# Expert results in two buffers per half of the columns, 31 instead of 32 weight slots, and the last pair stored by 256 columns

## The chip, the core and the metric

The kernel runs as one program on one core of a Trainium2 chip. The core has a matrix engine (TensorE, PE in the profile, with its weight loads as PEld), three engines for elementwise work (VectorE or DVE, ScalarE or ACT, GpSimd or POOL) and SyncE (SP), whose queue issues the DMA transfers here. Matmul operands are read from SBUF and results land in PSUM, which has eight banks. The metric is the device time of one execution in microseconds, lower is better.

## What is computed

One layer of a diffusion backbone over 512 latent tokens of 1024 features: a token mixer (neighbourhood attention beside a bidirectional RWKV-7 scan), then a mixture of 32 experts, of which each token uses two. The change is in the expert part:

```python
combine = jnp.sum(jax.nn.one_hot(expert_id, N_EXPERTS, dtype=jnp.float32) * top_w[..., None], axis=1)
out = jnp.zeros_like(hf)
for e in range(N_EXPERTS):
    he = jax.nn.silu(hf @ w1[e]) * (hf @ w3[e])
    out = out + combine[:, e:e + 1] * (he @ w2[e])
...
x = x + mod_x[5] * hier_moe(...)
```

Here `w1[e]` and `w3[e]` are 1024 by 512 and `w2[e]` is 512 by 1024, all float32, so each expert has 6 MB of weights, which are read once.

## The kernel before, in words

Each expert has a room of 64 tokens. `moe_phase` (line 1541) runs 16 pairs of experts, `moe_pair` for each. The two experts of a pair fill 128 rows, 64 each. For every second pair `gather` (1743) collects the features of four experts: TensorE multiplies one-hot matrices `OH` by the tokens (`pga`), and ACT moves the banks to `HS`. Pair 0 finds much of its gather already done.

A pair then runs so. The first products with `w1` and `w3` go to two PSUM banks (`ph`, 64 matmuls in the profile's count). ACT computes `hid = silu(ph)` and DVE multiplies it by the second bank, line 1798. TensorE transposes it (`pth`), and ACT copies it to `hT`. `turned` (1837) makes the pair's scatter matrix `oht` and its weights `cs` from a table (`pbp`, `pbc`). The products with `w2` (`py`) come in two halves of 512 columns. For each half `result` (1853) has DVE multiply by `cs` and the gate to `yv` (a tile `HS` for half 0, `hid` for half 1), ACT round it to `yh`, and DVE compute the rest `yl = yv - yh`, so that the two together carry float32 through matmuls in a shorter format. `scatter` (1864) multiplies `oht` by `yh` and `yl` for each of four token tiles (`psc`, eight matmuls for a half) and DVE adds the bank to the residual `x`. The pool `PM` has one buffer for each name, so one `yh` and one `yl`; both halves use them.

The scatter of a pair is a generator, `s.todo`, which the next pair advances: half 0 (four steps, line 1799) behind that pair's product `hid`, half 1 (line 1805) behind `hT`. So TensorE runs: `ph` of the next pair, scatter of half 0, `pth`, scatter of half 1, `pbp`/`pbc`, `py`. TensorE and DVE keep the order in which the program is written in this stage, as do the weight loads on SP; ACT's order is set by a scheduler.

Weights come by `wload2` (1708), two transfers of 512 KB at a time. There are `sum(RING)` slots in six pools, taken in turn, so load n takes the slot of load n - 32 and waits until TensorE has used it; it also waits for the load eight before it. The last pair (`e == 30`) takes its columns in four parts of 256, and `scatter` stores finished columns of `x` when the last token tile of a part is added and the part's end is a key of `STORES`: two transfers for each store, one for each half of the rows of the grid.

Of the kernel before, what the change touches and what calls it, by code (L numbers as in the profile page):

```python
# [9 lines left out]
F32R = mybir.dt.float32r  # L10
# [180 lines left out]
OUT_ORD = ('scalar',)  # L191
MOE_ORD = ('vector',)
LAST_PARTS = (256, 256, 256, 256)
STORES = {512: 0, 768: 512, 1024: 768}
PEND = 8.32  
AHEAD = 4
LATE = (4, 8, 12)
RING = (6, 15, 3, 4, 2, 2)
EARLY = 6


# [25 lines left out]
class K:  # L227
# [1480 lines left out]
    def wload2(s, e, m, b):  # L1708

        two = []  # L1710
        for h in range(2):
            n = s.nload % sum(RING)
            s.nload += 1
            r = next(r for r in range(len(RING)) if n < sum(RING[:r + 1]))
            src = s.A[m][e + h, b]
# [57 lines left out]
    def moe_pair(s, PM, e, batch):  # L1773

        nc = s.nc
        q = e // 2 % 2
        last = e == 30
        if q == 0:
            OH, s.HS, begun = batch
            if s.HS is None:  # L1780
                s.HS = s.features_room(PM)
            s.all(s.gather(OH, s.HS, begun))
        HS = s.HS[:, :, 128 * q:128 * q + 128]
        hs = [slice(64 * h, 64 * h + 64) for h in range(2)]
        hh = []
        for m in ('w1', 'w3'):
            ph = s.ps(tag='ip', name="ph")
            for b in range(4):
                ws = s.wload2(e, m, b)
                for k in range(2):  # L1790
                    kt = 2 * b + k
                    for h in range(2):
                        s.mm(ph[hs[h], :], HS[:, kt, hs[h]], ws[h][:, k], kt == 0, kt == KT - 1)
            hh.append(ph)
        ws = [s.wload2(e, 'w2', b) for b in range(4)]
        hid = PM.tile([128, 512], F32, name="hid")
        s.act(hid, hh[0], AF.Silu)
        nc.vector.tensor_tensor(hid, hid, hh[1], ALU.mult)
        s.some(s.todo, 4)
        pt = s.ps(tag='nt', name="pth")  # L1800
        for f in range(4):
            s.tr(pt[:, 128 * f:128 * f + 128], hid[:, 128 * f:128 * f + 128])
        hT = PM.tile([128, 512], F32, name="hid").rearrange("p (a b) -> p a b", a=4)
        s.act(hT.rearrange("p a b -> p (a b)"), pt)
        s.all(s.todo)
        oht, cs = s.turned(PM, e, HS[:, 4:8])
        batch = (s.moe_batch(PM, e // 4 + 1), None, None) if q and not last else None

        c0 = 0
        parts = LAST_PARTS if last else (512, 512)  # L1810
        for z, n in enumerate(parts):
            c = slice(c0, c0 + n)
            d = slice(c0 % 512, c0 % 512 + n)
            py = s.ps((128, n), tag=('ip', 'ip', 'rm', 'nt')[z], name="py")
            for a in range(c0, c0 + n, 256):
                for f in range(4):
                    for h in range(2):
                        s.mm(py[hs[h], a - c0:a - c0 + 256], hT[:, f, hs[h]], ws[a // 256][h][:, f], f == 0, f == 3)
            if d.start == 0:
                y2 = [PM.tile([128, 512], F32R, name=x) for x in ("yh", "yl")]  # L1820
            yh, yl = [t[:, d] for t in y2]

            yv = HS[:, c0 // 128:(c0 + n) // 128] if last or z == 0 else PM.tile([128, 512], F32, name="hid").rearrange("p (a b) -> p a b", a=4)
            s.result(yv, py, cs, s.mod5[c0 // 512][:, d], yh, yl)
            if last:
                s.all(s.todo)
            new = s.scatter(oht, c, yh, yl, last)
            s.todo = new if last or z == 0 else s.chain(s.todo, new)
            c0 += n
        s.all(s.todo) if last else None  # L1830
        return batch
# [32 lines left out]
    def scatter(s, oht, c, yh, yl, last=False):  # L1864

        for i in range(4):
# [5 lines left out]
            s.nc.vector.tensor_tensor(x, po, x, ALU.add)  # L1872
            if last and i == 3 and c.stop in STORES:
                s.store(slice(STORES[c.stop], c.stop))
            yield
# [119 lines left out]
```

## Time and profile before

| | us |
|---|---|
| Median of 3 runs (lowest, highest) | 1272.22 (1269.41, 1273.02) |
| Profiled execution, its time | 1272.23 |
| Its span in the trace | 1270.4 |
| TensorE matmul busy | 1133.3 (89%) |
| TensorE weight loads busy | 775.4 (61%) |
| DVE busy | 660.3 (52%) |
| ACT busy | 393.6 (31%) |
| GpSimd busy | 253.3 (20%) |

The expert stage begins at about 722 us of the span. The shares are means over stages of different kinds, so they don't tell what bounds this stage; that is read from its own waits and its timeline. Where an engine is idle, the profile names what it was waiting for. All instructions that a helper records have one line number (242 for matmuls, 212 for most others), so rows are told apart by their tiles, as `out<-in`. Times of matmuls overlap: one starts before the one ahead of it has ended.

### The profile page before, as it was taken

The numbers are of one execution on the slowest core, as the hardware profiler recorded it, in microseconds if no ns is written. First come the engines' busy times: TensorE is split into PE (matmuls) and PEld (weight loads), VectorE is DVE, ScalarE is ACT, GpSimd is POOL, SyncE is SP. The second block draws the span as 40 slices with busy tenths as digits, with TensorE's granted clock in tenths as the row PEclk, the third lists the DMA queues.
The fourth block names the chain that finished last, engine by engine and source line by source line (L and its number), as shares of the span: only waits on it lengthen the run. The fifth ranks groups of instructions, "written<-read, shape, count | busy, mean of one in ns | idle before, by whom it ended". The sixth has DMA issues, their size and how long they took to land.

```text
span 1270.4 us, 23663 instructions
## 1 busy us (share of the span) xinstructions
PE 1133.3 (89%) x9545; PEld 775.4 (61%) x9546; DVE 660.3 (52%) x1461; ACT 393.6 (31%) x743; POOL 253.3 (20%) x277
## 2 busy tenths in 40 slices
PE   4899998997968989999979899999999999998995
PEld 2677766865737868887757545454645545454644
DVE  5745597598899335544787513333333231313335
ACT  3533534545444446553223401020111101010101
POOL 0655364544343100202350300000000000000000
PEclk9999988996889889999989899999999999999998
DMA  9434634744534786643438599999989899999932
GB/s 368 152 125 146 196 130 132 203 143 128 139 109 147 198 239 195 197 101 105 122 119 346 177 410 406 376 367 367 405 330 410 328 395 367 369 361 375 354 155 68
DMA packets 148221, 309.98 MB, mean 244 GB/s; under 512 B 32260, under 2 KB 70020, under 8 KB 148109
## 3 DMA queue, kind: packets, MB, share of 16 engines
q1 hardware_dynamic: 143324, 306.08, 67.9%
q10 hardware_dynamic: 4752, 2.36, 0.6%
q8 instruction: 76, 1.25, 0.4%
q14 instruction: 37, 0.30, 0.1%
q0 software_dynamic: 32, 0.00, 0.0%
HBM read 283.22 MB, written 25.17 MB: 243 GB/s over the span
## 4 chain that ended last, share of the span: by engine, by line


## 5 line engine op out<-in xcount | busy, mean ns | idle before, releaser
L242 PE MATMUL ph<-wt,HS 128*64 128x512 f32 x1024 | 222.9, 593 | 0.0
L212 DVE TENSOR_TENSOR yl<-hid,yh 128x512 fp32r<-128x512 f32 x15 | 10.4, 692 | 287.8 <-ACT yh L212 287.8
L242 PEld LDWEIGHTS ph<-wt,HS 128*64 128x64 f32 x1024 | 72.9, 137 | 139.3 <-issue 131.0
L242 PE MATMUL py<-wt,hid 128*64 128x256 f32 x1024 | 114.7, 381 | 0.0
L212 POOL CAST two<-sel 128x128 fp32r<-128x128 f32 x32 | 8.5, 293 | 495.6 <-PE pbc L242 490.2
L242 PEld LDWEIGHTS py<-wt,hid 128*64 128x64 f32 x1024 | 71.9, 137 | 41.4 <-issue 6.3
L212 POOL TENSOR_TENSOR wlo<-wraw,whi 128x512 fp32r<-128x512 f32 x54 | 74.5, 1382 | 71.5 <-ACT whi L212 69.6
L242 PE MATMUL ipn<-whi,hth 128*128 128x256 f32 x256 | 80.2, 313 | 5.8 <-DVE vs L212 4.6
L212 ACT ACTIVATE yh<-hid 128x512 fp32r<-128x512 f32 x15 | 9.4, 629 | 243.8 <-PE psc L242 243.8
L212 DVE TENSOR_TENSOR x<-psc,x 128x512 f32<-128x512 f32 (+1 forms) x136 | 79.9, 649 | 1.5
L242 PE MATMUL ip<-hth,whi 128*128 128x512 f32 (+1 forms) x200 | 75.9, 380 | 0.3 <-ACT nr L212 0.2
L242 PE MATMUL ipn<-wlo,hth 128*128 128x256 f32 x256 | 75.4, 295 | 0.0
L242 PE MATMUL ipn<-whi,htl 128*128 128x256 f32 x256 | 75.3, 294 | 0.0
L242 PE MATMUL ip<-htl,whi 128*128 128x512 f32 (+1 forms) x200 | 72.6, 363 | 0.7 <-DVE htl L212 0.7
L242 PE MATMUL ip<-hth,wlo 128*128 128x512 f32 (+1 forms) x200 | 72.2, 361 | 0.0
L242 PE MATMUL psc<-yh,oht 128*128 128x512 f32 (+1 forms) x136 | 67.0, 496 | 1.3 <-DVE x L212 0.9
L242 PE MATMUL psc<-yl,oht 128*128 128x512 f32 (+1 forms) x136 | 63.6, 471 | 0.0
L242 PEld LDWEIGHTS ipn<-whi,hth 128*128 128x128 f32 x256 | 52.2, 204 | 17.7 <-issue 14.7
L242 PE MATMUL pga<-OH,xl 128*128 128x256 f32 x240 | 60.2, 291 | 2.2 <-POOL xl L212 2.2
L242 PE MATMUL pga<-OH,xh 128*128 128x256 f32 x240 | 61.0, 294 | 1.0 <-DVE OH L212 1.0
L212 DVE TENSOR_TENSOR tmp<-Mc,Tc 128x30 f32<-128x30 f32 (+14 forms) x120 | 54.2, 452 | 4.7 <-ACT Tc L212 3.2
L212 DVE TENSOR_TENSOR Tc<-Tc,tmp 128x30 f32<-128x30 f32 (+14 forms) x120 | 52.4, 436 | 2.0
(352 smaller groups left out, 2291.0 us busy)
## 6 DMA issues: line engine op xcount, KB each, us to landing
wt<-in_w_dram SPq DMA_DIRECT2D x384, 512.0 KB
wm<-in_wmod_dram SPq DMA_DIRECT2D x48, 512.0 KB
wraw<-in_w_in_dram SPq DMA_DIRECT2D x30, 256.0 KB
wraw<-in_w_na_dram SPq DMA_DIRECT2D x24, 256.0 KB
BKj<-BKd SPq DMA_DIRECT2D x12, 512.0 KB
BKd<-BK SPq DMA_DIRECT2D x12, 384.0 KB
ARz<-ARd SPq DMA_DIRECT2D x16, 256.0 KB
wo<-in_w_out_dram SPq DMA_DIRECT2D x16, 256.0 KB
```

The costliest lines, as they stand in the source:

```text
L212: i = f(*a, **k)
L242: i = s.nc.tensor.matmul(out, l, r, start=start, stop=stop)
```

## The change

`yh` and `yl` get two buffers each, so that half 0 and half 1 alternate between them. The room comes from the fourth pool of weight slots, which has three slots instead of four, so load n waits for load n - 31. `STORES` gets a key for column 256, so that the first 512 columns are stored in two parts.

```diff
-STORES = {512: 0, 768: 512, 1024: 768}
+STORES = {256: 0, 512: 256, 768: 512, 1024: 768}
...
-RING = (6, 15, 3, 4, 2, 2)
+RING = (6, 15, 3, 3, 2, 2)
...
             if d.start == 0:
-                y2 = [PM.tile([128, 512], F32R, name=x) for x in ("yh", "yl")]
+                y2 = [PM.tile([128, 512], F32R, name=x, bufs=2) for x in ("yh", "yl")]
```

The rows of TensorE, DVE and GpSimd come in the same order as before. On ACT, the order around a gather in the expert stage was this before (`yh<-HS` is half 0's rounding, `yh<-hid` is half 1's, `hid<-ph` is Silu and `hid<-pth` the copy to `hT`):

```order
L212 ACTIVATE hid<-pth 128x512
L212 ACTIVATE yh<-HS 128x512
L212 ACTIVATE HS<-pga,modv,sc_6889 128x256 x8
L212 ACTIVATE yh<-hid 128x512
L212 ACTIVATE hid<-ph 128x512
```

In the changed kernel the same place on ACT reads:

```order
L212 ACTIVATE hid<-pth 128x512
L212 ACTIVATE yh<-HS 128x512
L212 ACTIVATE yh<-hid 128x512
L212 ACTIVATE HS<-pga,modv,sc_6889 128x256 x8
L212 ACTIVATE hid<-ph 128x512
```

The rounding of half 1 has moved ahead of the eight moves of gathered features. This is so at all seven gathers behind pair 0.

On SP, the end of the expert stage (the last two weight loads, the stores, and the check whether an expert has more than 64 tokens) differs so:

```order
 L212 DMA wt_11671<-in_w_dram 128x1024
 L212 DMA wt_11673<-in_w_dram 128x1024
-L212 DMA out_dram<-x_4959 64x4x512 x2
-L212 DMA out_dram<-x_4959 64x4x256 x4
+L212 DMA out_dram<-x_4959 64x4x256 x8
 L1881 TENSOR_LOAD cmax
 L1882 COMPARE_AND_BRANCH
```

Two stores of 512 columns have become four of 256; they stay behind all weight loads.

## Rows read from the trace of the kernel before

**Rows 1.** page, 40 slices of the span: GB/s that the DMA engines moved in each

```profile
GB/s 368 152 125 146 196 130 132 203 143 128 139 109 147 198 239 195 197 101 105 122 119 346 177 410 406 376 367 367 405 330 410 328 395 367 369 361 375 354 155 68
```

**Rows 2.** waits, 722 to 1262: engine, line, waited for; us in total, times, longest

```profile
PE pth L246 <- DVE hid L212: 39.4, 16, 2.9
...
PEld ph L242 <- DMA wt<-in_w_dram: 3.4, 12, 0.3
```

**Rows 3.** timeline, one pair: start us, us, engine; in brackets idle before, releaser

```profile
896.58 0.50 PE L242 MATMUL psc<-yh,oht 128*128 128x512 f32 x1
...
898.83 0.63 ACT L212 ACTIVATE yh<-hid 128x512 fp32r<-128x512 f32 x1 [17.88 <-PE psc L242]
...
899.49 0.69 DVE L212 TENSOR_TENSOR yl<-hid,yh 128x512 fp32r<-128x512 f32 x1 [15.75 <-ACT yh L212]
...
900.22 0.60 ACT L212 ACTIVATE hid<-ph 128x512 f32<-128x512 f32 x1 [0.76 <-DVE yl L212]
...
900.85 0.69 DVE L212 TENSOR_TENSOR hid<-hid,ph 128x512 f32<-128x512 f32 x1 [0.66 <-ACT hid L212]
...
901.45 1.88 DVE L212 TENSOR_TENSOR x<-psc,x 128x512 f32<-128x512 f32 x3
...
901.59 0.66 PE L246 MATMUL pth<-cst,hid 128*128 128x128 f32 x4 [2.90 <-DVE hid L212]
```

**Rows 4.** windows: us; PE, PEld, DVE, ACT, POOL busy; granted clock, DMA share, GB/s

```profile
901.60:902.60 1.00, 0.96 (x5) 0.70 (x6) 1.00 (x2) 0.32 (x1) 0.00 (x0) 0.96 1.01 401
902.70:905.90 3.20, 3.20 (x9) 2.54 (x8) 3.06 (x7) 0.18 (x1) 0.00 (x0) 0.50 1.02 408
906.10:940.00 33.90, 31.34 (x204) 18.37 (x203) 7.69 (x14) 5.93 (x11) 0.53 (x2) 1.00 0.92 363
722.00:1257.80 535.80, 495.46 (x2856) 272.11 (x2855) 175.26 (x288) 70.69 (x125) 7.96 (x30) 0.95 0.88 345
```

**Rows 5.** timeline, pair 0

```profile
729.22 0.60 ACT L212 ACTIVATE hid<-ph 128x512 f32<-128x512 f32 x1 [4.67 <-PE ph L242]
...
735.95 0.66 PE L246 MATMUL ptb<-cst,byt 128*128 128x128 f32 x4
...
736.89 0.66 PE L246 MATMUL pth<-cst,hid 128*128 128x128 f32 x4 [0.29 <-DVE hid L212]
```

**Rows 6.** waits of SP's DMA queue, 722 to 1257

```profile
SPq L212 <- PE ph L242: 114.9, 83, 8.9
...
SPq L212 <- PE py L242: 110.4, 51, 8.8
```

**Rows 7.** windows of the weight stream

```profile
658.30:735.00 76.70, 68.22 (x447) 47.47 (x449) 50.84 (x189) 29.87 (x58) 16.90 (x21) 0.90 0.71 268
...
735.00:765.00 30.00, 26.53 (x157) 12.32 (x153) 7.85 (x12) 3.08 (x6) 0.53 (x2) 1.00 1.03 410
...
1219.50:1257.80 38.30, 35.65 (x216) 19.11 (x213) 16.14 (x32) 3.70 (x7) 0.00 (x0) 0.96 0.00 1
...
658.30:1219.50 561.20, 515.02 (x3027) 296.09 (x3029) 209.97 (x446) 93.96 (x172) 24.86 (x51) 0.94 0.92 360
```

**Rows 8.** page, DMA issues: count, KB each

```profile
wt<-in_w_dram SPq DMA_DIRECT2D x384, 512.0 KB
```

**Rows 9.** timeline, last pair and stores

```profile
1224.34 13.90 PE L242 MATMUL ph<-wt,HS 128*64 128x512 f32 x64
...
1252.74 1.41 DVE L212 TENSOR_TENSOR x<-psc,x 128x256 f32<-128x256 f32 x4
...
1255.58 1.95 PE L242 MATMUL py<-wt,hid 128*64 128x256 f32 x16
...
1257.85 1.36 SPq L212 DMA_DIRECT2D out_dram<-x  x2
...
1259.05 2.73 DVE L212 TENSOR_TENSOR x<-psc,x 128x256 f32<-128x256 f32 x8
...
1263.64 1.98 SPq L212 DMA_DIRECT2D out_dram<-x  x2
```

## The prediction

> **What bounds the kernel now.** I start with the slices of the page [rows 1]. Slices 24 to 38 are mostly the expert stage, in which the weight loads move some 330 to 410 GB/s. The first question is whether TensorE or the weight stream sets the pace there. The waits of that stage answer it [rows 2]: the matmul side of TensorE stood for 39.4 us, 16 times, before the transposes `pth` of the hidden tile, and its weight loads stood for only 3.4 us because weights had not landed. The queue that issues the loads, on the other hand, waited 225 us for TensorE to give slots back [rows 6]. So weights are early, and TensorE is the bound, with one hole per pair.
>
> The timeline of one pair shows the hole [rows 3]. TensorE starts the scatter of half 0 at 896.58, and `pth` at 901.59 after 2.90 us without work, so the eight scatter matmuls are over at 898.69. In it four instructions run one after another: ACT `yh` of half 1 (898.83), DVE `yl` (899.49), ACT's Silu into `hid` (900.22), DVE's product `hid` (900.85, 0.69 long). ACT had waited 17.88 us for `psc` by then: the one `yh` buffer was still read by half 0's scatter, which TensorE runs only after the next pair's 64 `ph` products. DVE keeps program order, so the product stood behind `yl`.
>
> The windows by clock show a second cost [rows 4]. A microsecond behind the hole the clock falls to 0.50 (the 1.2 GHz level of the two): 902.7 to 905.9 reads 0.50, the microsecond before it 0.96, the stretch from 906.1 to 940 reads 1.00. TensorE is busy all through the slow stretch, 3.20 of 3.20 us, so the fall adds half of its length to the chain.
>
> **The change, part by part.** *Two buffers for `yh` and `yl`.* Half 1 no longer takes the buffer that half 0's scatter reads; its own was last read by the previous pair's half-1 scatter, before the `py` products that feed it. `yh` and `yl` then run right behind `py`, under 13.90 us of `ph` products [rows 9]. ACT can take Silu as soon as the w1 products end, half way through `ph`. What is left behind `ph` is the product `hid` alone. Pair 0, which has no scatter in front of it, already runs like that [rows 5]: Silu at 729.22, in the middle of `ph`; TensorE's next work (four other transposes) at 735.95, and `pth`, which still waits for the product, at 736.89: 0.94 us after `ph`. In later pairs the eight scatter matmuls cover 2.11 us, which hides 0.94 with 1.17 to spare. The cover would hold even if Silu came late (0.60 more).
>
> So 15 of the 16 holes go; pair 0 keeps its 0.29 us [rows 5]. 39.4 - 0.3 = **39.1 us**. The fall of the clock comes 15 times, each behind a hole; by the windows it is between 3.2 and 3.5 us long, I take 3.4. Half of 3.4 times 15 is **25.5 us**. As a check, a mean clock of 0.95 over 535.8 us [rows 4] is a loss of 26.8, within the rounding of that figure. I take the fall to go with its hole, as nothing else in the stage precedes one; if it doesn't, the price is a rival below.
>
> *What is late next?* After `pth` the half-1 scatter needs the banks that DVE's additions empty: DVE starts them 0.9 us behind `ph`, at 0.63 each (1.88 for three [rows 3]), and bank i is free at about 1.6+0.63i; TensorE asks for it at about 2.8+0.46i, so by the fourth pair of matmuls the margin is still 0.7 us. I cost this at nothing; if it fails, it costs at most some 0.7 us per pair.
>
> *ACT's new order.* Where a gather follows, `yh` of half 1 stands ahead of the eight `HS` evacuations. It needs only `py` and DVE, and TensorE hardly waits for `HS` at all, so I cost it at nothing. The upper end is 0.63 x 7 = 4.4 us, if in each of the seven gathers behind pair 0 every `HS` came late by a whole `yh` and TensorE waited for it.
>
> *One slot less (31 instead of 32).* Each load waits for a slot one load younger. In the trace of before that costs nothing: the last weights land at 1219.5 (from then on 1 GB/s) [rows 7] and the last `py` group starts at 1255.58 [rows 9], 36 us later. With TensorE faster, it matters. A load is 512 KB [rows 8], and at the 410 GB/s of 735 to 765 [rows 7] takes 1.279 us; 24 of them need 30.7 us per pair. TensorE's time per pair was 34.2 us (ten pairs from 896.58 [rows 3] to the end of the last `ph` at 1238.24 [rows 9], five of them with a gather) and falls by 2.6 + 1.7 to 29.9, so the lead shrinks by 0.8 us per pair. The tightest place is the last pair's `ph`: its end at 1238.24 [rows 9] moves by 14 x (2.61+1.70) to 1177.9, and its last eighth, which needs load 376 of 384, starts at 1176.2. Until 735, 268 GB/s x 76.7 us [rows 7] is 39 loads, of which I count 38 as landed; 735 + 338 x 1.279 + 1.28 for the lost slot is 1168.6. The lead left is 7.6 us, so the slot costs nothing, but the margin is thin: the stream must hold (1176.2-735-1.28)/338 = 1.302 us per load, **403 GB/s**. The lower bound of the slot's price is nothing, the upper a load per pair, 15 x 1.28 = 19 us, if the stream is the bound throughout; as the row gives 410, I take the lower.
>
> *Stores of the last pair.* Eight of 256 KB instead of two of 512 and four of 256. The first two are free to go when the additions of the first 256 columns end, 1252.74+1.41, instead of 1257.85 [rows 9]. SP has issued all loads by then. Before, the last two issues began at 1263.64, though the last additions ended at 1261.78: SP's queue was behind. With 512 KB gone 3.7 us earlier the last two can start between 1261.8 and 1263.6: a gain of nothing to 1.9 us. I take **1.5 us**, near the upper end, since the queue then has a quarter of its bytes behind it.
>
> Sum, against the profiled execution of 1272.23 us (span 1270.4; the median of the runs shown is 1272.22, so no correction): 39.1 + 25.5 + 1.5 = 66.1, which gives **1206.1 us**.
>
> **The rivals.**
> *The half-level clock stays.* Something else than the hole could bring it down, the change to `psc` and `pth` shapes for one. Against it: one fall per hole, and none around pair 0. Time: 1206.1 + 25.5 = 1231.6. Chance 0.06.
>
> *The stream becomes the bound.* Then the hole moves from `pth` to the weights of the last pairs. For it: the mean over 658.3 to 1219.5 is only 360 GB/s [rows 7], and the margin above is 2%. Against it: the stream was held back by slots for 225 us of that time [rows 6], and unhindered it went at 410. At 360 GB/s (1.456 us), 346 loads after 735 end at 1238.8; from the last group's start at 1255.58 to the end are 16.7 us, less 1.5 for the stores: 1254. Near the margin, at 391 GB/s (1.341 us), it is 1214. Chance 0.07 for more than 1218. The Trainium skill (DMA: Bandwidth & Descriptors, Specifications) has a limit of about 358 GB/s of HBM for one core. By that rule a load takes 1.465 us, an estimate from its figure, and the end is near 1257; the trace's 410 GB/s goes against the rule on this chip.
>
> *The change doesn't do what it says.* If half 1 still waited for half 0's scatter, all stays, 1271 with the stores. ACT's order in the change speaks against it: `yh` now stands ahead of `HS`, which would not be possible with a wait that ends behind them. Chance 0.03.
>
> *Slower: the stream starves.* With 31 slots, every halt of TensorE's weight use fills the ring a load earlier, the stream stops, and the time is not made up. Its place is the `ph` products behind a gather. It ends slower than before when a load takes over (1272.23-16.7+1.5-735)/346 = 1.509 us on average, under 347 GB/s. The slowest slices of the stage, 328 and 330 GB/s [rows 1], would be 1.59 us and 1300 us in all. Against it: those slices are halts for slots that TensorE gives back late, and it gives them back sooner now. Chance 0.04.
>
> **How the numbers follow.** The forecast has 0.80. Its own range: at the low end the stores give 1.9 and a run is as much below the median as the lowest shown (1269.41, 2.8 below), which is 1203, and two more for holes that I have not priced, 1201. At the high end the stores give nothing, `HS` costs 4.4, and the stream runs at about 391 GB/s (8 us): some 1218 to 1220; I take 1218, as all three together are unlikely. The rivals' 0.20 lies outside. A measurement of this kernel can tell about 0.3% (3.8 us) from no change. Faster: 0.80 + 0.06 + 0.07 = 0.93; same 0.03; slower 0.04.
>
> **What would show it.** Right: no wait of `pth` for DVE beyond pair 0; ACT's Silu in the middle of `ph` in every pair; a granted clock of 1.00 from 740 to the last pair; DMA near 410 GB/s until about 1170, and the queue's waits for TensorE down from 225 us to some tens. The last load should land some 12 us or more before the last `py` group. Wrong: waits of TensorE for weights that add up to several us, first in the last pairs; half-level stretches without a hole; `psc` waiting for DVE's additions in every pair; the last stores issued no sooner after the last addition than now.

## The result and the profile after

The changed kernel takes 1203.38 us (median of 4 runs, 1202.46 to 1205.15), the kernel before 1271.91 us beside it. The ratio is 0.9465, with a 95% interval of 0.9448 to 0.9483. The forecast was 1206.1 us in a range of 1201 to 1218.

The profiled execution took 1203.45 us, with a span of 1201.7. First the waits of the expert stage. The rows are waits of TensorE's matmul side, then of its weight loads for the weights (engine, line, waited for: us in total, times, longest).

```profile
PE pth L246 <- DVE hid L212: 0.3, 1, 0.3
...
PEld ph L242 <- DMA wt<-in_w_dram: 8.9, 28, 1.1
```

Against [rows 2], the wait of the transposes has gone from 39.4 us to the 0.3 of pair 0, and the waits for weights have grown from 3.4 to 8.9 us.

The timeline of one pair, on ACT, DVE and TensorE, shows how:

```profile
1042.51 0.63 ACT L212 ACTIVATE yh<-hid 128x512 fp32r<-128x512 f32 x1 [2.76 <-DVE hid L212]
...
1043.17 0.69 DVE L212 TENSOR_TENSOR yl<-hid,yh 128x512 fp32r<-128x512 f32 x1 [0.69 <-ACT yh L212]
...
1048.59 0.60 ACT L212 ACTIVATE hid<-ph 128x512 f32<-128x512 f32 x1 [5.45 <-PE ph L242]
...
1055.53 0.69 DVE L212 TENSOR_TENSOR hid<-hid,ph 128x512 f32<-128x512 f32 x1 [11.66 <-PE ph L242]
...
1057.28 0.60 PE L246 MATMUL pth<-cst,hid 128*128 128x128 f32 x4
```

In [rows 3] these five stood in a row, within 3 us, behind half 0's scatter. Now `yh` and `yl` of half 1 run at the start of the `ph` products and Silu in the middle of them. The product waits for nothing but `ph`, and `pth` has no idle time ahead of it.

The windows (us; PE, PEld, DVE, ACT and POOL busy; granted clock, DMA share, GB/s) show the clock and the stream:

```profile
735.00:1150.00 415.00, 414.25 (x2551) 231.58 (x2548) 151.96 (x248) 63.59 (x113) 7.49 (x28) 1.00 1.03 409
...
1182.50:1188.00 5.50, 4.96 (x39) 3.21 (x36) 3.91 (x10) 0.88 (x3) 0.00 (x0) 1.00 0.01 4
```

The granted clock is 1.00 for 415 us without a break (0.95 over the stage in [rows 4]), and TensorE is busy for 414.25 of them. The DMA engines move 409 GB/s through the same stretch. Unhindered they did 410 before [rows 7], so the stream has no time left either. The last weights land at about 1182.5; the last `py` group starts at 1188.46, below, so it has a lead of 6 us where it had 36.

SP's queue hardly waits for TensorE any more: 24 us in these two rows, where [rows 6] has 225 (33 and 228 with the smaller rows). It now waits for the loads themselves, each for the one eight before it:

```profile
SPq L212 <- DMA wt<-in_w_dram: 305.2, 341, 1.5
SPq L212 <- PE ph L242: 19.6, 41, 5.4
...
SPq L212 <- PE py L242: 4.0, 12, 1.2
```

The end, on TensorE, DVE and SP:

```profile
1159.77 13.21 PE L242 MATMUL ph<-wt,HS 128*64 128x512 f32 x58
1173.19 1.93 PE L242 MATMUL ph<-wt,HS 128*64 128x512 f32 x6 [0.21 <-DMA wt<-in_w_dram]
...
1187.03 1.36 SPq L212 DMA_DIRECT2D out_dram<-x  x2
...
1188.46 1.95 PE L242 MATMUL py<-wt,hid 128*64 128x256 f32 x16
...
1191.77 2.73 DVE L212 TENSOR_TENSOR x<-psc,x 128x256 f32<-128x256 f32 x8
...
1193.86 2.90 SPq L212 DMA_DIRECT2D out_dram<-x  x3
```

The first two stores start at 1187.03, before the last `py` group; in [rows 9] they started after it. From that group to the end of the span it is 13.2 us, where it was 14.8. The first two rows show a new wait: in the last pair TensorE stands for weights inside `ph`.

Where the 68.7 us of span went can be read from the timelines of both kernels. I take the start of the first matmul of one kind and that of the next, and add up over the 15 pairs behind pair 0 (the third row over all 16):

| us | before | after | `fill_before`, below | `yh_only`, below |
|---|---|---|---|---|
| scatter of half 0 and the hole, `psc` to `pth` | 70.9 | 29.5 | 71.0 | 64.8 |
| transposes, `pth` to `psc` | 10.4 | 5.3 | 10.4 | 9.9 |
| table products, `pbp` to `py` | 11.0 | 9.0 | 9.0 | 12.0 |
| scatter of half 1, `psc` to `pbp` | 49.5 | 28.8 | 34.1 | 44.3 |
| `ph` products, `ph` to `psc` | 207.9 | 209.3 | 207.9 | 207.9 |
| stage: first `ph` to last `py` group | 533.5 | 466.3 | 517.0 | 524.1 |

The stage accounts for 67.2 us and the end for 1.6. The stage begins at the same time in both (722.06 and 722.18). In other profiled executions it began anywhere between 718 and 727 us, before the part that the change touches; below I therefore use the stage's own length as well as the run's time.

### The profile page after: what moved, and what is told of

Same layout as the page of the kernel before. It is cut to its first block, busy times and chain, and to the rows that moved or that the text cites. A ratio compares the mean times of both kernels' runs of the same rounds, so it can differ in the third digit from the quotient of the medians.

```text
span 1201.7 us, 23662 instructions
## 1 busy us (share of the span) xinstructions
PE 1105.2 (92%) x9545; PEld 761.2 (63%) x9546; DVE 658.4 (55%) x1461; ACT 393.5 (33%) x743; POOL 249.6 (21%) x277
## 4 chain that ended last, share of the span: by engine, by line
PE 68%; DVE 21%; DMA 6%; ACT 2%; issue 2%; POOL 1%; SPq 0%; ACTq 0%; DVEq 0%; POOLq 0%
PE ph L242 17%; PE py L242 9%; PE psc L242 7%; PE ipn L242 5%; PE pga L242 5%; PE ip L242 5%; DVE tmp L212 4%; DVE Tc L212 4%; PE pgr L242 2%; DMA wt<-in_w_dram 2%; PE pm L242 2%; PE acc L242 2%; PE pr L242 2%; PE pon L242 1%; PE ppt L246 1%
## 5 line engine op out<-in xcount | busy, mean ns | idle before, releaser
L212 DVE TENSOR_TENSOR hid<-hid,ph 128x512 f32<-128x512 f32 x16 | 11.0, 688 | 249.3 <-PE ph L242 249.3
L242 PEld LDWEIGHTS ipn<-whi,hth 128*128 128x128 f32 x256 | 51.4, 201 | 17.8 <-issue 14.8
L212 DVE TENSOR_TENSOR tmp<-Mc,Tc 128x30 f32<-128x30 f32 (+14 forms) x120 | 56.8, 473 | 4.8 <-ACT Tc L212 3.2
L242 PE MATMUL psc<-yh,oht 128*128 128x512 f32 (+1 forms) x136 | 54.6, 405 | 1.2 <-DVE x L212 0.8
L242 PEld LDWEIGHTS ip<-hth,whi 128*128 128x128 f32 x200 | 39.9, 199 | 21.0 <-issue 15.7
L212 ACT ACTIVATE hid<-pth 128x512 f32<-128x512 f32 x16 | 9.6, 599 | 132.7 <-PE pth L246 132.7
```

The lines of the kernel that those rows point to most:

```text
L212: i = f(*a, **k)
L242: i = s.nc.tensor.matmul(out, l, r, start=start, stop=stop)
```

## The experiments

**The lost slot alone.** The kernel before with

```diff
-RING = (6, 15, 3, 4, 2, 2)
+RING = (6, 15, 3, 3, 2, 2)
```

> The kernel before with 31 slots and nothing else. Theory (weights were some 30 us early, so the slot costs nothing while TensorE has its holes): 1272 us, within 1 us of before. Rival (the ring is full behind every gather, and each halt of the stream comes a load earlier and isn't made up): up to 15 loads of 1.28 us, 1285 to 1291 us.

Measured: 1273.25 us beside 1274.62, a ratio of 0.9982 (0.9966 to 0.9998), and a stage of 532.6 us. The wait of `pth` is the same 39.4 us. The slot costs nothing while TensorE has its holes; the rival is out.

**The stores alone, and the buffers alone.** The kernel before with the new `STORES`, and the changed kernel with the old:

```diff
-STORES = {512: 0, 768: 512, 1024: 768}
+STORES = {256: 0, 512: 256, 768: 512, 1024: 768}
```

> The kernel before with the stores by 256 columns alone. Theory: 1.5 us less than before, 1270.4 us. Rival (the last store waits for the last addition only, the stores ahead of it are hidden anyway): 1272 us.

> The changed kernel with the stores of before (two of 512 columns first). Theory (the two buffers carry all but the end): 1203.4 + 1.5 = 1205 us, 0.948 of before. Rival (the earlier stores carry more, since they empty the DMA queue ahead of the last ones): 1207 us or more.

Measured: the stores alone 1271.89 us (0.9977 of before, 0.9956 to 0.9997), the buffers alone 1206.69 us (0.9467, 0.9445 to 0.949). Later the buffers alone and the changed kernel ran again on one chip:

> The changed kernel once more, on the same chip as the two that follow, so that differences of 1 to 2 us can be read. Theory: 0.9465 of before, 1203 us where before is at 1272.

> The changed kernel with the stores of before, beside the changed one. Theory (the stores by 256 give 1.5 us): 1.5 us above the changed kernel. Rival (they gave nothing, and the shorter tail is chance): the same to within 0.5 us.

Measured: 1205.93 us for the changed kernel (0.9478, 0.9464 to 0.9493) and 1207.56 for the buffers alone (0.9494, 0.9474 to 0.9514). The two differ by 1.6 us, as expected, though their intervals overlap. The profiles are sharper: from the last addition to the end of the span it is 7.0 to 7.2 us in the seven profiles with stores by 256 on SP's queue. With the stores of before it is 8.1 and 8.6 in the two of the buffers alone, 8.6 in the kernel before and with the lost slot alone, and 9.6 in `fill_before`, below. So the stores are worth about 1 to 1.5 us and the buffers all the rest.

**The hole parted from the clock.** The kernel before, with useless matmuls in the hole:

```diff
         s.some(s.todo, 4)
+        if e:
+            idle = s.ps(tag='rm', name="idle")
+            for _ in range(10):
+                s.mm(idle, s.table[:, 0:128], s.table)
```

> The kernel before with ten matmuls of no use (into a bank that is read by nobody) between half 0's scatter and the transposes, from pair 1 on: 2.3 us of the hole is filled with work. It parts the hole from the fall of the clock. Theory (the fall goes with the idle time): the clock stays at 1.00 in the whole stage, the hole costs what it did, and 25 to 28 us go: 1244 to 1247 us. Rival 1 (the fall has another cause, the kind of matmul behind the hole): 1272 us with 15 stretches at 0.50. Rival 2 (the filler comes on top): 1272 + 15 x 2.3 = 1306 us.

Measured: 1254.28 us beside 1274.62 (0.983, 0.9798 to 0.9862), 20 us less, and a stage of 517.0, 16.5 less. The stage is the better measure here: this profiled execution reached it 4 us earlier than that of before, which the filler, standing behind that point, can't bring about. Fifteen times ten more matmuls make this kernel faster. The waits of TensorE and the window over the stage:

```profile
PE pth L246 <- DVE hid L212: 5.2, 16, 0.6
```

```profile
722.00:1235.00 513.00, 505.84 (x2970) 278.80 (x2966) 171.67 (x282) 68.07 (x121) 7.96 (x30) 1.00 0.92 361
```

What idles is now 5.2 us instead of 39.4, and the clock is 1.00 throughout: the fall does go with the hole. But it was worth 16 to 20 us and not the 25 to 28 expected. The table says where most of the rest is. Half 1's scatter still takes 34.1 us against 28.8 in the changed kernel. (The transposes take 10.4 us as before, against 5.3, so their 5 us hang on the hole and not on the clock.) This row of the same kernel gives the reason for the scatter (2.7 us, 11 times, in the kernel before):

```profile
PEld psc L242 <- DVE x L212: 12.6, 45, 0.3
```

As the product is late here too, so are DVE's additions behind it, and TensorE waits for the banks that they empty. In the kernel before, the slow clock had covered that.

**The same filler in the changed kernel.**

> The same ten matmuls of no use in the changed kernel, where no hole is left for them. Theory (TensorE is the bound of the stage up to the last pair): they come on top, 15 x 2.3 = 34.5 us less the 1.5 us for which the last pair now waits for weights: 1236 us, and the stream gets halts again. Rival (the weight stream alone is the bound now): they are hidden, 1203 to 1210 us.

Measured: 1238.67 us (0.9733, 0.9653 to 0.9814); the stage is 499.2 us, 32.9 longer than in the changed kernel. The ten matmuls that were free before now come on top in full (34.5 less the 1.5 of the last pair's wait). TensorE is a bound of this stage.

**Less work for TensorE.** The changed kernel without the low halves of the tokens in the gathers behind pair 0, so half of these products is left out:

```diff
-            s.mm(pg[:, z], s.xh[i][:, c], r, i == 3 and z == 0, False)
-            s.mm(pg[:, z], s.xl[i][:, c], r, False, i == 0 and z == 1)
+            both = len(tiles) < 4
+            s.mm(pg[:, z], s.xh[i][:, c], r, i == 3 and z == 0, not both and i == 0 and z == 1)
+            if both:
+                s.mm(pg[:, z], s.xl[i][:, c], r, False, i == 0 and z == 1)
```

> The changed kernel without the matmuls of the low halves of the tokens in the seven gathers behind pair 0: half of the gather's products is left out, and TensorE has about 20 to 27 us less to do; the weights are the same. Theory (the stream has no time left either, the last pair already waits for it): the last weights land where they did, near 1182, and the time is 1203, at most 2 us to either side, with waits for weights of about 20 us in all. Rival (TensorE alone is the bound): 1176 to 1183 us.

Measured: 1203.42 us (0.9456, 0.9367 to 0.9545), no difference that two runs can show; the stage is 467.5 us. Seven gathers are shorter by 3.85 us each, 26.9 in all, and the `ph` products are longer by 28.4. The groups of the stage say why: weight loads of `ph` that waited for weights, 41.8 us, twice the 20 expected.

```profile
L242 PEld LDWEIGHTS ph<-wt,HS 128*64 128x64 f32 x1006 | 78.2, 136 | 160.4 <-issue 110.8 <-DMA wt<-in_w_dram 41.8 <-ACT HS L212 4.0
```

So the stream is a bound as well. The two run out at the same point: work added on TensorE costs its full time, work taken away gives nothing.

**Fewer slots.** The changed kernel with 24:

```diff
-RING = (6, 15, 3, 3, 2, 2)
+RING = (6, 8, 3, 3, 2, 2)
```

> The changed kernel with 24 slots instead of 31. Theory (the stream is at its limit at the end, and each slot less starts it 1.28 us later): 1203.4 + 7 x 1.28 = 1212 us, with waits for weights in the later pairs. Rival (TensorE alone is the bound, slots are plenty): 1203 us. Second rival (fewer slots make the stream halt again and again): over 1225 us.

Measured: 1214.67 us (0.9545, 0.9466 to 0.9623), a stage of 475.2, 8.9 longer, which is the time of seven loads (9.0). In this kernel a slot is worth one load, 1.28 us, once and not per pair, on the mean of these seven.

**Only `yh` doubled.**

```diff
-                y2 = [PM.tile([128, 512], F32R, name=x, bufs=2) for x in ("yh", "yl")]
+                y2 = [PM.tile([128, 512], F32R, name=x, bufs=b) for x, b in (("yh", 2), ("yl", 1))]
```

> The changed kernel with two buffers for yh and one for yl. Theory (four links in a row make the hole, yh, yl, Silu and the product): only the first link leaves it, 0.63 + 0.07 us of each hole of 2.6; yl of half 1 still waits for the scatter of half 0 and holds Silu, which writes into the tile that yl reads. So 15 x 0.7 = 10 us less than before with the clock still falling, and the stores' 1.5: 1260 us; if the shorter hole no longer brings the clock down, 1233 us. Rival (the product and Silu don't wait for yl, so yh alone was the cause): 1204 us.

Measured: 1259.34 us (0.9896, 0.9798 to 0.9994), a stage of 524.1, 9.4 less than before. One hole of it:

```profile
868.35 0.69 DVE L212 TENSOR_TENSOR yl<-hid,yh 128x512 fp32r<-128x512 f32 x1 [22.98 <-PE psc L242]
869.08 0.60 ACT L212 ACTIVATE hid<-ph 128x512 f32<-128x512 f32 x1 [15.71 <-DVE yl L212]
869.70 0.69 DVE L212 TENSOR_TENSOR hid<-hid,ph 128x512 f32<-128x512 f32 x1 [0.66 <-ACT hid L212]
...
870.45 0.65 PE L246 MATMUL pth<-cst,hid 128*128 128x128 f32 x4 [2.20 <-DVE hid L212]
```

The chain has lost its first link and keeps the other three: `yl` waits for half 0's scatter, and Silu waits for `yl`. The total came as expected; its parts less so. The hole shrank by 0.4 us and not by 0.7, and 3 us of the gain come from the clock, which fell behind 11 of the 15 holes.

**Stores from two queues.** The changed kernel with

```diff
+            q = s.nc.scalar if h and c.start >= 512 and c.stop - c.start == 256 else s.nc.sync
-            s.nc.sync.dma_start(o[:, ::1 - 2 * h], s.x1[64 * h:64 * h + 64, :, c])
+            q.dma_start(o[:, ::1 - 2 * h], s.x1[64 * h:64 * h + 64, :, c])
```

> The changed kernel with one of the two transfers of each of the last two parts issued by ACT's queue instead of SP's, where eight issues of 0.6 to 1.4 us stand in a row at the end. Theory (SP's queue is what the last store waits for): the last issue begins 0.8 us earlier, 1202.5 us, 0.5 to 1 us below the changed kernel. Rival (the transfers themselves are what is slow there): no difference.

Measured: 1208.12 us (0.9485, 0.9461 to 0.9509), no gain. The last two issues did begin together, at 1198.80, 0.03 us behind the last addition, but from there to the end it is 7.5 us where it was 7.2. So an earlier issue alone does not bring the end forward; what in the transfers takes the time was not tried. No version here beats the changed kernel.

## Why the prediction was right

**The hole.** It was one chain of four links, held by the one buffer each of `yh` and `yl`, and it is gone: the wait of `pth` fell from 39.4 to 0.3 us, as the step said. The term of 39.1 us was too small. By the table the hole took 41.5 us between scatter and transposes and another 5.0 in the transposes, which take 0.36 us in an engine that hasn't stopped and 0.69 behind a hole.

**The clock.** The fall goes with the hole, as forecast: `fill_before` keeps the late product, fills the idle time and has no fall. The term of 25.5 us was too large. The slow stretches lie in two rows of the table, half 1's scatter and the table products. Together these are 17.4 us shorter in `fill_before` and 22.7 in the changed kernel. So the fall alone cost 16 to 20 us, and DVE's additions would have held half 1's scatter for 5 us anyway. The changed kernel gets these 5 us too, as its product comes early. So the two terms erred in opposite directions, and that their sum of 64.6 is so near the 67.2 of the stage is in part luck.

**What is late next.** The additions cost nothing in the changed kernel, as worked out: half 1's scatter takes 1.92 us, and no row shows TensorE waiting for them except once, in the last pair (0.8 us, where it was 0.9 before). ACT's new order costs nothing either; all seven gathers take the 7.82 us that most took before.

**The slot and the stream.** That a slot is free was right for the kernel before. In the changed one it is worth about 1.3 us by `slots_24`; the two buffers with 32 slots were not run. The step that was off is the lead: 7.6 us were worked out for the last pair's `ph`, and TensorE waited there for 1.4 us (209.3 against 207.9). Two sizes failed. TensorE came to that place some 4 us sooner than calculated, as the holes and what hangs on them were worth more: without the wait this `ph` would have ended at 1173.7. And load 376, the last that `ph` needs, came later: 1168.6 was worked out, and by the trace's record of its semaphore it was complete at 1173.15. TensorE's second row above starts at 1173.19. The prediction had counted bytes, and by bytes 376 loads had landed at 1170.0. But eight loads share the stream, as SP's queue holds a load back only until the one eight before it has landed, and each is some ten us on its way (load 376 was issued at 1162.97). By 1173.15 the bytes of 378 loads had landed, so part of the later ones came ahead of its own last bytes. The place was right. The condition was not: 403 GB/s should have been enough, and the stream held 409 and TensorE still waited.

**The rivals.** The half-level clock did not stay. The stream did become a bound, but only in the last pair. The change does what it says. And nothing starved, as the stream held 409 GB/s for 415 us. The Trainium skill (DMA: Bandwidth & Descriptors, Specifications) has a limit of about 358 GB/s for one core in its table; this program ran on one core and moved 409, so the trace differs from the table, and it decides.

**The stores.** 1.5 us were expected; the runs on one chip gave 1.6, and the ends of the profiles about 1 to 1.5.

**The signs that were named.** Silu in the middle of `ph`, a clock of 1.00 and a stream near its full rate until the end all came. The last weights land 6 us ahead of the last `py` group and not the 12 or more that I named. Of the signs of being wrong one came in small: the waits for weights in the last pair.

## What to carry to other kernels

When a tuned stage has one short hole per step, list the instructions inside it and ask of each what it waits for; here a chain of four small ones hung on two tiles of 2 KB per partition, `yh` and `yl` (`yh` alone gave 9 us of the stage's 67), behind an engine that keeps program order. Before trading a slot of prefetch for such a buffer, work out how far ahead the transfers still are when the hole is gone: count a load as there when its own transfer is complete, not when as many bytes have come. Here both resources run out at almost the same point, so the next gain needs fewer bytes and less TensorE work together; that was not tried. Useless work in the hole, and the same work in the kernel without it, tells in two runs what the clock is worth beside the idle time and whether the engine is the bound.

## What was not expected of the hardware

Ten useless matmuls per pair made the kernel before 20 us faster, since TensorE did not idle and stayed at the 2.4 GHz level. The granted clock fell behind all 15 holes of 2.6 to 2.9 us, behind 11 of the 15 of 2.2 us in `yh_only`, and behind none of the 0.3 to 0.6 us that are left in `fill_before`. These two windows of `yh_only` show both cases. The first is behind the hole at 870.45, shown above, the second behind this one; the clock is 1.00 from 876 to 967:

```profile
900.37 0.65 PE L246 MATMUL pth<-cst,hid 128*128 128x128 f32 x4 [2.21 <-DVE hid L212]
```

```profile
871.90:875.10 3.20, 3.20 (x8) 2.10 (x7) 3.20 (x6) 0.00 (x0) 0.00 (x0) 0.50 1.03 410
903.00:906.00 3.00, 3.00 (x24) 1.90 (x25) 2.90 (x6) 0.00 (x0) 0.53 (x2) 1.00 1.03 410
```

Why a hole of the same length brings the clock down at one place and not at another was not tried.
